# A fixed order for every engine in the MLP's down projection, with its loads issued by ScalarE

## The chip, the cores and the metric

The kernel runs on one core of a Trainium2 chip. A core has TensorE (PE in the profile: matmuls; PEld: the loads of its stationary operand), VectorE (DVE), ScalarE (ACT), GpSimd (POOL) and SyncE (SP), each with its own stream of instructions, and 16 DMA engines that move data between DRAM and the on-chip memories. The metric is the device time of one execution in microseconds (us).

## The reference, cut to what matters

A hybrid decoder block on x of 512 tokens by 2048 channels in float32: a token mixer (gated linear attention and differential attention, one output projection), then a gated MLP with a causal convolution, with norms around both. The change touches the MLP alone.

```python
def conv_ffn(h, w_ffn_in, conv_w, conv_b, w_ffn_out):        # D_FF = 5632
    up = h @ w_ffn_in                                        # 2048 -> 2 * 5632
    a, b = up[..., :D_FF], up[..., D_FF:]
    a = (conv_w[0] * a_pad[:, 0:S] + conv_w[1] * a_pad[:, 1:S + 1]
         + conv_w[2] * a_pad[:, 2:S + 2] + conv_b)
    return (jax.nn.gelu(a, approximate=True) * b) @ w_ffn_out   # 5632 -> 2048

h = rmsnorm(x, ffn_pre_norm[l])
f = conv_ffn(h, w_ffn_in[l], conv_w[l], conv_b[l], w_ffn_out[l])
x = x + rmsnorm(f, ffn_post_norm[l])
```

## The kernel before, in words

**Products of float32 in three matmuls.** A matmul reads fp32r, a rounded float32. Each operand is therefore two fp32r numbers, hi (the rounded value) and lo (what the rounding left), and a product is hi·hi + hi·lo + lo·hi. Weights pass through in *granules*: a block of 128 x 1024 float32 (512 KB) is loaded into a buffer named `raw` or `rt` (four of each), ACT copies it to hi (L136) and DVE subtracts to get lo (L137). The hi and lo go to one of three slots of a tile named `ring`, or to a pair named `xhi`, `xlo`, which every fourth granule of the down projection uses. `ring` has two placements, LEVEL and APART, which shift the halves by some columns; a half in one placement reaches into the neighbour's slot in the other. The up projection uses APART, the down projection LEVEL. Activations are split the same way by ACT and DVE (L149, L150) into pieces of the tiles `ah` and `al`.

**Seven products for eight.** Hidden channels come in eleven groups of 512. Of each pair of groups 2c+1 and 2c+2 (c = 0 to 4), the down projection is computed as 2 x 2 block products in the Strassen and Winograd form: seven products where eight would be. A *unit* is one pair c and one half `cb` of the output columns, so there are ten of them, `downs[0]` to `downs[9]`. The segments of a unit are called x0, z0, y0, z1, x1, y1, y2; each has two granules of 12 matmuls of 128 x 512 (L1024 to L1026). The units overlap: the order of segments is x0 of the next unit ahead of y2 of this one, and its z0 behind. The up projection is made of such units too (L927 to L929, matmuls of 128 x 256).

The sums that the form needs are made on the way. Of weights: the block loaded as `t` feeds x0 and z0 (and gets another block added by an accumulating DMA that POOL issues, L876), then DVE adds `b22` (L892) for y0, and `b21` (L910) for y2; `b22` feeds z1 and, after another accumulating DMA, y1; `b21` feeds x1. Of activations: DVE makes four sums of a finished pair of groups (`token_sums`, L995), SP stores them and three plain quarters to DRAM (`sd0s`, `sd0a` for pair 0, and so on), and `prepare` loads each back into a tile `st` and splits it. The names of these seven are a11, s5, s2, s3, a12, s7, a22, in the order of the segments x0, z0, y0, z1, x1, y1, y2.

Each segment's result is added from PSUM to `acc` or `accp` in SBUF by DVE (L1032), or written by ACT for the first pair (L1030). After the last unit six operations of 128 x 1024 (L1119) add `accp` into `acc`. The eleventh group (group 0, computed first, kept in DRAM as `ud0`) has no partner; its down projection is 16 plain parts of 12 matmuls (L1139 to L1141) at the end, each added (L1143), squared (L1148), scaled (L1152), and the rows are finished with the norm and the residual (L1172). The residual is loaded from `x1d`, 4 MB in four pieces, into `ah` and `al` once these are free.

**What sets the order.** The code calls the segments of the units in order; the framework's scheduler places the instructions on each engine by a simulated timeline and by the order of the code. All loads (`raw`, `rt`, `st`) are issued by SP (L48), and SP's order, too, is the scheduler's. Only the last parts of the last group stand in an order written out by hand, inside `tc.manual_schedule(engines=IN_ORDER)`, where PE, ACT, DVE and POOL take their instructions as the code emits them.

Of the kernel before, what the change touches and what calls it, by code (L numbers as in the profile page):

```python
# [17 lines left out]
P = 128  # L18
# [17 lines left out]
def hybrid_layer(ctx: ExitStack, tc: tile.TileContext, x, attn_pre_norm, w_in, w_alpha_up, b_alpha,  # L36
# [813 lines left out]
    def load_t(src, a):  # L850
        raw = rp.tile([P, GR], F32, name="rt", tag="rt", bufs=4)
        dma(raw.rearrange("p (a b) -> p a b", a=a), src)
        return raw
# [77 lines left out]
    held = {}  # L931

    def up_unit(gi, br):
# [10 lines left out]
        def out(seg, b):  # L944
# [20 lines left out]
            elif seg == "y2":  # L965
                tt(st["u0"][:, :, T[1]], v, st["p1"], ALU.add)
                if br == 0:
                    activate(0)
                else:
                    product(0)  # L970
                    token_sums(gi, st["u0"], st["u1"])
# [13 lines left out]
    def token_sums(gi, u0, u1):  # L985
        c, i = (gi - 1) // 2, (gi - 1) % 2
        T = [slice(0, 256), slice(256, 512)]
        a11, a21, a12, a22 = u0[:, :, T[0]], u0[:, :, T[1]], u1[:, :, T[0]], u1[:, :, T[1]]

# [3 lines left out]
        def add(n, x, y, op):  # L993
            t = fp.tile([P, 2, 256], F32, name=n, tag="sum", bufs=2)
            tt(t, x, y, op)  # L995
            put(n, t)
            return t
# [4 lines left out]
        s5 = add("s5", a21, a22, ALU.subtract)  # L1002
        s2 = add("s2", s5, a11, ALU.subtract)
        add("s7", a11, a21, ALU.subtract)
        add("s3", s2, a12, ALU.add)
# [50 lines left out]
    for i, u in enumerate(ups):  # L1056
        nxt = ups[i + 1] if i + 1 < len(ups) else None
        if i == 0:
# [4 lines left out]
        if i == 0:  # L1063
            for h, r in enumerate(s7raw):
                split(up["s7"][0][:, h], up["s7"][1][:, h], r)
        if nxt is None:
            prepare(0, "a11")
        u.x1()
        if nxt is None:
            prepare(0, "s5")  # L1070
        u.y1()
        if nxt is not None:
            nxt.x0()
            u.y2()
            nxt.z0()
        else:
            downs = [down_unit(c, cb) for c in range(NG // 2) for cb in range(2)]
            downs[0].x0()
            prepare(0, "s2")
            u.y2()  # L1080
    accps = large_tile("accp")
    accp = [accps[:, :D // 2], accps[:, D // 2:]]
    acc = [large_tile(f"acc{t}") for t in (2, 3, 0, 1)]
    acc = acc[2:] + acc[:2]
    ssf = [few.tile([P, 4], F32, name=f"ssf{t}") for t in range(NT)]
    downs[0].z0()
    extra[0] = True
    for i, u in enumerate(downs):
        nxt = downs[i + 1] if i + 1 < len(downs) else None
        nc_ = (i + 1) // 2  # L1090
        first = i % 2 == 0
        last_cb = i % 2 == 1 and nxt is not None

        if first:
            prepare(i // 2, "s3")
        if i == 6:
            g3 = large_tile("g3")
            bcast_row(g3, ffn_post_norm[0])
        u.y0()
        if first:  # L1100
            prepare(i // 2, "a12")
        u.z1()
        if first:
            prepare(i // 2, "s7")
        u.x1()
        if first:
            prepare(i // 2, "a22")
        if last_cb:
            prepare(nc_, "a11")
        u.y1()  # L1110
        if last_cb:
            prepare(nc_, "s5")
        if nxt is not None:
            nxt.x0()
        else:
            for j in range(2):
                for half, c, op in ((1, 0, ALU.add), (1, 1, ALU.subtract), (0, 1, ALU.subtract)):
                    dst = acc[2 * half + j].rearrange("p (b c x) -> p b c x", b=2, c=2)[:, :, c, :]
                    tt(dst, dst, accp[j].rearrange("p (b x) -> p b x", b=2), op)  # L1119
        if last_cb:  # L1120
            prepare(nc_, "s2")
        u.y2()
        if nxt is not None:
            nxt.z0()

    place_w[0] = LEVEL


# [115 lines left out]
```

## Time and profile before

| | |
|---|---|
| median of 3 runs | 2150.28 us (2150.27 to 2150.32) |
| the profiled execution | 2150.54 us |
| its span, first to last instruction | 2148.8 us |
| mean granted TensorE clock | 0.997 |
| PE busy | 2108.8 us, 98% of the span |
| DVE busy | 1415.8 us, 66% |
| ACT busy | 900.2 us, 42% |
| POOL busy | 199.2 us, 9% |

All times below are counted from the span's start. The up projection ends and the down projection begins at about 1690 us; the down units run from there to about 2088, the last group's parts to about 2140, and the finishing of the rows to 2148.8. A row that ends in brackets says how long the engine was idle just before the instruction and what ended that idle time. A wait for several things is put down to the one that came last.

### The profile page before, as it was taken

What the parts mean: (1) busy time and instruction counts of PE and PEld (TensorE: products, weight loads), DVE (VectorE), ACT (ScalarE), POOL (GpSimd) and SP (SyncE); (2) the same over time, 40 slices, a digit from 0 to 9 for tenths busy, and PEclk for the clock granted to TensorE, in tenths of its full rate; (3) what the DMA queues carried; (4) which work ended last, traced back from release to release, by engine and by line L of the source; (5) the groups of instructions that cost most, each with busy time, mean ns of one, the idle gap of its engine ahead of it and who ended that gap; (6) DMA issues with size and microseconds to landing.
All of it is one profiled execution on the core that took longest, in us unless ns stands there. A gap on an engine that the chain in (4) does not pass through costs nothing.

```text
span 2148.8 us, 31859 instructions
## 1 busy us (share of the span) xinstructions
PE 2108.8 (98%) x13009; PEld 1874.8 (87%) x13009; DVE 1415.8 (66%) x1725; ACT 900.2 (42%) x1162; POOL 199.2 (9%) x242
## 2 busy tenths in 40 slices
PE   7999999999999999999999999999999899999998
PEld 6878888888888888899999999999999778887886
DVE  5345554443444237688778786787877778888887
ACT  4233332333343224344544553554454555444433
POOL 1000000000000001010111101111011111111100
PEclk9999999999999999999999999999999999999999
DMA  6322222223224235356775767758577777676653
GB/s 214 102 72 79 79 70 79 79 79 88 78 80 170 95 128 186 119 118 143 167 182 132 169 162 173 167 136 194 142 171 183 189 216 207 168 196 175 160 166 144
DMA packets 218471, 303.83 MB, mean 141 GB/s; under 512 B 11776, under 2 KB 155572, under 8 KB 216404
## 3 DMA queue, kind: packets, MB, share of 16 engines
q1 hardware_dynamic: 165204, 238.87, 33.2%
q0 software_dynamic: 53120, 62.92, 19.1%
q8 instruction: 102, 1.67, 0.3%
q14 instruction: 45, 0.37, 0.1%
HBM read 273.97 MB, written 27.79 MB: 140 GB/s over the span
## 4 chain that ended last, share of the span: by engine, by line
PE 54%; issue 37%; DMA 3%; POOL 3%; DVE 2%; ACT 1%; POOLq 0%; SPq 0%; DVEq 0%; ACTq 0%
PE bank L190 7%; PE bank L191 7%; PE bank L192 7%; PE bank L174 5%; PE bank L172 5%; PE bank L173 5%; PE bank L929 4%; PE bank L927 4%; PE bank L928 4%; POOL rt L876 2%; POOL raw L876 1%; PE bank L440 1%; DMA raw<-in_w_ffn_in_dram 1%; PE bank L508 1%; PE bank L539 1%
## 5 line engine op out<-in xcount | busy, mean ns | idle before, releaser
L137 DVE TENSOR_TENSOR ring<-raw,ring 128x1024 fp32r<-128x1024 f32 x305 | 371.7, 1221 | 354.0 <-ACT ring L136 349.6
L136 ACT ACTIVATE ring<-raw 128x1024 fp32r<-128x1024 f32 x305 | 322.7, 1060 | 594.2 <-PE bank L192 157.2
L929 PE MATMUL bank<-ah,ring 128*128 128x256 f32 x1280 | 353.5, 276 | 0.7 <-DVE ring L137 0.7
L927 PE MATMUL bank<-ah,ring 128*128 128x256 f32 x1280 | 353.3, 276 | 0.0
L928 PE MATMUL bank<-al,ring 128*128 128x256 f32 x1280 | 353.3, 276 | 0.0
L137 DVE TENSOR_TENSOR ring<-rt,ring 128x1024 fp32r<-128x1024 f32 x221 | 269.3, 1221 | 92.3 <-ACT ring L136 92.2
L136 ACT ACTIVATE ring<-rt 128x1024 fp32r<-128x1024 f32 x221 | 233.5, 1060 | 223.5 <-PE bank L928 151.5
L929 PEld LDWEIGHTS bank<-ah,ring 128*128 128x128 f32 x1280 | 240.3, 188 | 1.1 <-DVE ring L137 1.1
L928 PEld LDWEIGHTS bank<-al,ring 128*128 128x128 f32 x1280 | 240.3, 188 | 0.1
L927 PEld LDWEIGHTS bank<-ah,ring 128*128 128x128 f32 x1280 | 240.3, 188 | 0.1
L190 PE MATMUL bank<-ring,ah 128*128 128x512 f32 x600 | 236.9, 398 | 0.2 <-ACT ah L149 0.2
L191 PE MATMUL bank<-ring,ah 128*128 128x512 f32 x600 | 235.9, 394 | 0.0
L192 PE MATMUL bank<-ring,al 128*128 128x512 f32 x600 | 235.1, 394 | 0.0
L172 PE MATMUL bank<-ah,ring 128*128 128x512 f32 (+1 forms) x512 | 195.9, 383 | 1.9 <-ACT ring L136 1.9
L174 PE MATMUL bank<-ah,ring 128*128 128x512 f32 (+1 forms) x512 | 194.2, 380 | 0.0
L173 PE MATMUL bank<-al,ring 128*128 128x512 f32 (+1 forms) x512 | 194.1, 379 | 0.0
L1025 PE MATMUL bank<-ring,ah 128*128 128x512 f32 x424 | 166.7, 393 | 8.8 <-DVE ring L137 8.8
L1026 PE MATMUL bank<-ring,al 128*128 128x512 f32 x424 | 165.8, 391 | 0.0
L1024 PE MATMUL bank<-ring,ah 128*128 128x512 f32 x424 | 158.2, 391 | 2.4 <-ACT ring L136 2.1
L192 PEld LDWEIGHTS bank<-ring,al 128*128 128x128 f32 x600 | 113.2, 189 | 24.2 <-DVE al L150 0.3
L191 PEld LDWEIGHTS bank<-ring,ah 128*128 128x128 f32 x600 | 113.3, 189 | 23.8 <-DVE ring L137 0.5
L190 PEld LDWEIGHTS bank<-ring,ah 128*128 128x128 f32 x600 | 113.2, 189 | 23.7 <-ACT ah L149 0.6
(260 smaller groups left out, 4063.4 us busy)
## 6 DMA issues: line engine op xcount, KB each, us to landing
raw<-in_w_in_dram SPq DMA_DIRECT2D x96, 512.0 KB, 3.7
raw<-in_w_ffn_in_dram SPq DMA_DIRECT2D x96, 512.0 KB, 5.1
raw<-in_w_ffn_out_dram SPq DMA_DIRECT2D x48, 512.0 KB, 6.7
rt<-in_w_ffn_in_dram SPq DMA_DIRECT2D x40, 512.0 KB, 5.9
rt<-in_w_ffn_in_dram POOLq DMA_DIRECT2D x40, 512.0 KB, 6.2
raw<-in_w_ffn_in_dram POOLq DMA_DIRECT2D x40, 512.0 KB, 6.9
raw<-in_w_o_dram SPq DMA_DIRECT2D x32, 512.0 KB, 3.7
rt<-in_w_ffn_out_dram SPq DMA_DIRECT2D x20, 512.0 KB, 7.3
```

What stands on the lines that cost most here:

```text
L136: act(hi, raw, AF.Copy)
L137: tt(lo, raw, hi.bitcast(F32), ALU.subtract)
L172: mm(o, wh, ah[:, t0:t1, kk, :], start=st, stop=False)
L173: mm(o, wh, al[:, t0:t1, kk, :], start=False, stop=False)
L174: mm(o, wl, ah[:, t0:t1, kk, :], start=False, stop=sp)
L190: mm(banks[t], ah[:, t, s, :], w[0][:, k, :], start=st, stop=False)
L191: mm(banks[t], ah[:, t, s, :], w[1][:, k, :], start=False, stop=False)
L192: mm(banks[t], al[:, t, s, :], w[0][:, k, :], start=False, stop=sp)
L927: mm(o, wh, sh[:, :, kk, :], start=start and kk == 0 and n == 0, stop=False, **NOW)
L928: mm(o, wh, sl[:, :, kk, :], start=False, stop=False, **NOW)
L929: mm(o, wl, sh[:, :, kk, :], start=False, stop=kk == HK - 1, **NOW)
L1025: mm(b[j], sh[:, o:o + P], w[1][:, q, :], start=False, stop=False, **NOW)
```

## The change

From the last up unit's x1 on, through all ten down units and two of the last group's 16 parts, everything is emitted by a new function, `run_in_order`, inside `manual_schedule(IN_ORDER)`. It walks over a list of granules; before the matmuls of granule i it makes the halves of all granules up to two ahead (i < 10) or three ahead (from then on), and behind the matmuls it calls what `hooks` holds for that granule: loads, sums, splits, the combination. What was a method of a unit (`x0` to `y2`, `more`) is now a place in that table. In detail:

- Loads of `t` (L852), `b22` and `b21` (L102) from the second down unit on, and loads of `st` (L1101) from the second pair on, are issued by ACT, one per granule. Those of the first unit and the first pair stay on SP.
- `prepare` falls into two steps, the load and the split, each with its own granule. Those of a11 and s5 of the first pair are called ahead of the region.
- The last `token_sums` is spread over four granules of the first down unit (L1002 now).
- The six combining operations become twelve of half the width (still L1119), half of them inside the last unit and half behind it.
- The loads and splits of the last group's activations move up, to units 4 and 5 and to the last unit. The weights of its first parts are made inside the region, and its first two parts stand ahead of the last y2.
- `ring` changes from APART to LEVEL once, at a granule where the spare pair lies between the two.
- `b21` of the last up unit is loaded ahead of the region.

The core of the diff:

```diff
-    def load(src, a):
+    def load(src, a, by=None):
         raw = wpool.tile([P, GR], F32, name="raw", tag="raw", bufs=4)
-        dma(raw.rearrange("p (a b) -> p a b", a=a), src)
+        (by or nc.sync).dma_start(out=raw.rearrange("p (a b) -> p a b", a=a), in_=src)
...
+    def prepare_parts(c, n, by):
+        got = []
+
+        def first():
+            got.append(small_tile("st"))
+            by.dma_start(out=got[0], in_=sd[c][n].rearrange("p g x -> p (g x)"))
+
+        def second():
+            split(piece(ah, *place[n]), piece(al, *place[n]), got[0])
...
+    def run_in_order(u, order, ahead):
+        gran = [(v, seg, g) for v, seg in order for g in range(2)]
+        ready, nxt = {}, [0]
...
+        def make(i):
+            v, seg, g = gran[i]
+            turn[0] += 1
+            place_w[0] = APART if i < late else LEVEL
+            if v is None:
+                gr0.append(ffn_out_granule(0, 0, g, extra[i]))
+                return
+            raw = getattr(v, SOURCE[seg][1])[g]
+            ready[i] = granule(None, v.a, raw, spare=extra[i])
+            j = {"x0": 1, "z1": 1}.get(seg)
+            if j:
+                nc.gpsimd.dma_start(out=raw.rearrange("p (a b) -> p a b", a=v.a), in_=v.block(0, j, g),
+                                    accum_op=ALU.add)
+
+        for i, (v, seg, g) in enumerate(gran):
+            while nxt[0] < len(gran) and nxt[0] <= i + (1 if nxt[0] == late else ahead(i)):
+                make(nxt[0])
+                nxt[0] += 1
+            if v is None:
+                for t in range(2 * g):
+                    ffn_out_part(whole, gr0, t, 0)
+                continue
+            op = SOURCE[seg][0]
+            if g == 0 and seg[1] == "0":
+                v.banks[seg[0]] = v.chain(seg[0])
+            v.prods(v.banks[seg[0]], op, g, ready.pop(i), seg[1] == "0")
+            if g:
+                v.out(seg, v.banks[seg[0]])
+            for f in hooks.pop((v, seg, g), ()):
+                f()
...
+        for d, v in enumerate(downs):
+            order += [(v, s) for s in ("z0", "y0", "z1", "x1", "y1")]
+            order += [(downs[d + 1], "x0") if d + 1 < len(downs) else (None, "last"), (v, "y2")]
...
+            for w, name, where in ((nxt, "t", (("z0", 0), ("y0", 1))), (nxt, "b22", (("x1", 0), ("x1", 1))),
+                                   (v if d else None, "b21", (("y2", 0), ("y2", 1)))):
+                for g in range(2) if w else ():
+                    at(before if name == "b21" else v, *where[g], lambda w=w, name=name, g=g: load_g(w, name, g, nc.scalar))
...
+    with tc.manual_schedule(engines=IN_ORDER):
+        run_in_order(u, order, lambda i: 2 if i < 10 else 3)
+    for k in range(3):
+        combine(1, k)()
```

What this does to the engines' orders is seen at three places. The first is SP's order where the up projection passes into the down projection; `st<-sd0s` are the loads of s5, s2, s3, s7 (in before the first of them is s5's), `st<-sd0a` those of a11, a12, a22. Before:

```order
L48 DMA raw<-in_w_ffn_in_dram 128x4x256 x2
L48 DMA rt<-in_w_ffn_out_dram 128x2x512 x2
L48 DMA st<-sd0a_6404 128x1024
L48 DMA raw<-in_w_ffn_out_dram 128x2x512 x4
L48 DMA st<-sd0s_6407 128x1024
L48 DMA st<-sd0s_6408 128x1024
L48 DMA st<-sd0s_6410 128x1024
L48 DMA st<-sd0a_6405 128x1024
```

The same place in the changed kernel:

```order
L102 DMA raw<-in_w_ffn_in_dram 128x4x256 x2
L852 DMA rt<-in_w_ffn_out_dram 128x2x512 x2
L48 DMA st<-sd0a_6404 128x1024
L48 DMA st<-sd0s_6407 128x1024
L1101 DMA st<-sd0s_6408 128x1024
L102 DMA raw<-in_w_ffn_out_dram 128x2x512 x2
L1101 DMA st<-sd0s_6410 128x1024
L102 DMA raw<-in_w_ffn_out_dram 128x2x512 x2
L1101 DMA st<-sd0s_6409 128x1024
```

The first two loads from `sd0s` moved from behind the four loads of down weights to ahead of them, and the later ones stand between these.

The second is DVE's order at the same passage; L137 makes a weight's lo half, L150 the lo half of a piece of the activations, L953, L955, L960 work on the up projection's result `u`, and L980 (L985 in the changed kernel) makes its product. Before, from the first split of a11 on:

```order
L150 TENSOR_TENSOR al<-st,ah 128x1024
L953 SCALAR_TENSOR_TENSOR u<-bank,p_14674 128x2x256
L137 TENSOR_TENSOR ring<-raw,ring 128x1024 x2
L955 TENSOR_TENSOR u<-u,bank 128x2x256
L137 TENSOR_TENSOR ring<-raw,ring 128x1024 x2
L137 TENSOR_TENSOR ring<-rt,ring 128x1024
L150 TENSOR_TENSOR al<-st,ah 128x1024
L137 TENSOR_TENSOR ring<-rt,ring 128x1024
L960 TENSOR_TENSOR u<-u,bank 128x2x256
L150 TENSOR_TENSOR al<-st,ah 128x1024
L980 TENSOR_TENSOR u<-u 128x1024
```

The changed kernel, from the same split on:

```order
L150 TENSOR_TENSOR al<-st,ah 128x1024
L953 SCALAR_TENSOR_TENSOR u<-bank,p_14674 128x2x256
L150 TENSOR_TENSOR al<-st,ah 128x1024
L137 TENSOR_TENSOR ring<-raw,ring 128x1024 x2
L955 TENSOR_TENSOR u<-u,bank 128x2x256
L137 TENSOR_TENSOR ring<-raw,ring 128x1024 x2
L1094 TENSOR_TENSOR rt<-rt,raw 128x1024 x2
L137 TENSOR_TENSOR ring<-rt,ring 128x1024
L150 TENSOR_TENSOR al<-st,ah 128x1024
L137 TENSOR_TENSOR ring<-rt,ring 128x1024
L960 TENSOR_TENSOR u<-u,bank 128x2x256
L985 TENSOR_TENSOR u<-u 128x1024
```

The second split (s5's) moved from between the lo halves of down weights (`ring<-rt`, the two granules of x0) to ahead of four lo halves of the up projection's last weights; two weight sums (L1094, L910 in before) now stand ahead of the first down granule, and a split (s2's) stands where s5's was.

The third is ACT's order in a steady unit. Before, it held copies alone:

```order
L149 ACTIVATE ah<-st 128x1024
L136 ACTIVATE ring<-rt 128x1024
L136 ACTIVATE ring<-raw 128x1024
L136 ACTIVATE xhi<-raw 128x1024
L136 ACTIVATE ring<-raw 128x1024 x3
L136 ACTIVATE xhi<-raw 128x1024
L136 ACTIVATE ring<-rt 128x1024 x3
```

In the changed kernel, near the start of the fifth pair, the loads stand between them:

```order
L136 ACTIVATE ring<-rt 128x1024 x2
L149 ACTIVATE ah<-st 128x1024
L1101 DMA st<-sd4a_6433 128x1024
L136 ACTIVATE ring<-rt 128x1024
L1101 DMA st<-sd4s_6437 128x1024
L136 ACTIVATE xhi<-rt 128x1024
L102 DMA raw<-in_w_ffn_out_dram 128x2x512
L136 ACTIVATE ring<-rt 128x1024
L102 DMA raw<-in_w_ffn_out_dram 128x2x512
L136 ACTIVATE ring<-rt 128x1024
L149 ACTIVATE ah<-st 128x1024
L852 DMA rt<-in_w_ffn_out_dram 128x2x512
```

Each of these loads waits, on ACT, until its buffer is free, and the copies behind it wait with it. At the end of SP's order the loads of `x1d_4800` and `x1d_4801` (2 MB) now stand directly ahead of the last group's weight loads: in before six `raw` loads of down weights, among them the last group's first, stood ahead of that pair.

More of the change, by code (lines that the diff above doesn't have):

```diff
@@ L848, in hybrid_layer, with load_t @@
     drain()
[L850 removed]
+    def load_t(src, a, by=None):
         raw = rp.tile([P, GR], F32, name="rt", tag="rt", bufs=4)
[L852 removed]
+        (by or nc.sync).dma_start(out=raw.rearrange("p (a b) -> p a b", a=a), in_=src)
         return raw
@@ L1066, in hybrid_layer @@
         if nxt is None:
-            prepare(0, "a11")
+            break
         u.x1()
-        if nxt is None:
-            prepare(0, "s5")
         u.y1()
[L1072 to L1082, printed above, removed]
```

193 lines of the change are left out of this document (127 added, 66 removed).

## The prediction

> **What bounds the kernel now.** I read the page's first part, then the windows by stage, then the idle time of the engine that is nearly always busy, then the rows of the engines it waited for.
>
> ```profile
> PE   2108.8 (98%) x13009; PEld 1874.8 (87%) x13009; DVE 1415.8 (66%) x1725; ACT 900.2 (42%) x1162; POOL 199.2 (9%) x242
> ```
> ```profile
> 1676.00:1690.00 14.00, 14.00 (x126) 14.00 (x125) 8.17 (x8) 5.79 (x6) 1.29 (x1) 1.00 0.99 243
> 1690.00:1740.00 50.00, 39.94 (x186) 31.91 (x185) 36.39 (x35) 24.36 (x28) 5.88 (x5) 0.93 0.89 260
> 1740.00:1777.00 37.00, 37.00 (x165) 30.64 (x164) 28.71 (x27) 24.29 (x29) 4.49 (x5) 1.00 0.71 190
> 1740.00:2088.00 348.00, 346.49 (x1523) 284.96 (x1522) 295.96 (x312) 166.34 (x169) 41.40 (x36) 1.00 0.68 177
> 2088.00:2149.00 61.00, 50.38 (x218) 40.25 (x216) 45.36 (x66) 18.46 (x39) 2.96 (x8) 0.96 0.40 149
> ```
>
> The span is 2148.8 us and PE is busy for 2108.8 of it, so all of PE's idle time is 40.0 us, and no matmul is added or removed. The second fence (us from the span's start, then length, then busy us and instructions of PE, PEld, DVE, ACT, POOL, then granted clock, DMA share, GB/s) covers the region of the change. PE is idle for 10.06 us in the 50 us of the passage from the up to the down projection, 1.51 us in the 348 us of the down projection, and 10.62 us at the end. A row with no gap in it (1740 to 1777, 165 matmuls) gives the cadence, 0.224 us per 512-wide matmul; 12 make a granule, 2.7 us, and 14 granules a unit, 37 us.
>
> ```profile
> PE bank L1025 <- DVE ring L137: 8.0, 3, 5.5
> PE bank L1024 <- ACT ring L136: 2.1, 3, 1.0
> ```
> ```profile
> 1678.79 6.62 SPq L48 DMA_DIRECT2D raw<-in_w_ffn_out_dram  x4
> 1685.46 10.09 SPq L48 DMA_DIRECT2D st<-sd0s  x3
> ```
> ```profile
> 1692.89 1.06 ACT L149 ACTIVATE ah<-st 128x1024 fp32r<-128x1024 f32 x1 [4.21 <-DMA st<-sd0s]
> ```
> ```profile
> 1688.72 1.23 DVE L137 TENSOR_TENSOR ring<-rt,ring 128x1024 fp32r<-128x1024 f32 x1 [3.70 <-ACT ring L136]
> 1693.98 1.23 DVE L150 TENSOR_TENSOR al<-st,ah 128x1024 fp32r<-128x1024 f32 x1 [4.04 <-ACT ah L149]
> 1695.12 1.22 DVE L137 TENSOR_TENSOR ring<-rt,ring 128x1024 fp32r<-128x1024 f32 x1
> ```
> ```profile
> 1696.99 0.63 PE L1026 MATMUL bank<-ring,al 128*128 128x512 f32 x1
> ...
> 1700.40 0.48 PE L1026 MATMUL bank<-ring,al 128*128 128x512 f32 x1
> ```
>
> These are PE's waits from 1560 to 1760 (us, times, longest), then SP's, ACT's, DVE's and PE's rows in the passage. The longest wait, 5.5 us, names a weight's lo half (L137), but that subtraction waited for nothing of its own: it starts at 1695.12 because the split before it in DVE's order (L150 at 1693.98) sat 4.04 us for ACT's half, which sat 4.21 us for the load of `s5` from `sd0s`. SP issued that load at 1685.46, behind four weight loads in its order, and it took 1692.89 − 1685.46 = 7.4 us. After the wait eight matmuls start in 1700.40 − 1696.99 = 3.41 us, 0.43 each and not 0.224; with the one at 1696.40, nine cost 1.9 us more, the clock's share of the wait. The Trainium skill, "TensorE: Matmul & The Clock Gate", Part 1, says that the clock halves after an idle window of about 3.4 us and returns after about as long a busy one; the row at 0.93 and these starts agree.
>
> A matmul's record lasts about 0.17 us beyond the next one's start, so each separate wait hides that much: with seven in the passage, 10.06 + 1.9 + 7 × 0.17 = 13.2 us are lost there. The same for the down projection, with about five waits: 1.51 + 0.85 = 2.4 us.
>
> ```profile
> PE bank L1025 <- DVE ring L137: 0.8, 2, 0.5
> PE bank L1140 <- DVE xlo L137: 0.8, 1, 0.8
> PE bank L1025 <- DVE xlo L137: 0.4, 2, 0.2
> PE bank L1140 <- DVE ring L137: 0.3, 1, 0.3
> PE bank L1024 <- DVE acc L1032: 0.3, 1, 0.3
> ```
>
> These are PE's waits from 1760 on; the two on L1140 belong to the last group, 1.1 us and with what is hidden 1.5. The rest of the 10.62 is the tail behind the last matmul.
>
> **The change, part by part.**
>
> *The passage.* The `s5` load goes out ahead of the raw loads that it stood behind, and its two splits stand in DVE's order ahead of the last up unit's x1, no longer between the halves of the first down granules. Both links of the chain above go: −13.2 us. What is late next: DVE.
>
> ```profile
> 1711.69 1.22 DVE L980 TENSOR_TENSOR u<-u 128x1024 f32<-128x1024 f32 x1
> 1715.47 0.69 DVE L995 TENSOR_TENSOR s<-u 128x512 f32<-128x512 f32 x1
> ```
>
> The windows give 36.39 us of DVE work in 50, and the same work (products and splits at 1.22, sums at 0.69) now has to fit beside a lo of 1.22 in every 2.7 us. Counting it off granule by granule, the up unit's x1 is short by about 0.3 us and the first y0 by 0.8 and 0.4: +1.5 us. From below this is 0 (all of it fits); from above 5, one wait like the old one without the half clock. I take 1.5. The ring's two placements, whose shifted buffers overlap, no longer alternate in the passage; the waits that this caused are among the seven, and the one switch left is part of the 1.5.
>
> *The steady units.*
>
> ```profile
> 2088.71 1.28 DVE L1032 TENSOR_TENSOR acc<-acc,bank 128x512 f32<-128x512 f32 x2
> 2089.91 2.35 DVE L1119 TENSOR_TENSOR acc<-acc,accp 128x1024 f32<-128x1024 f32 x2
> ```
>
> Per granule DVE does one lo (1.22), one output (L1032, 1.28 / 2 = 0.64) and the rest in splits and adds. Over the unit that is the 28.7 us of 37 in the row, and the new order deals it out so that no granule has over 3.5 us and the backlog never passes 0.9 us. Halves are made three granules ahead: 3 × 2.7 − 1.06 − 1.22 = 5.8 us of lead. So −2.4 us of waits goes and I leave 0.4 for what a queue in fixed order can't step around: −2.0. Ends: −2.4, and no gain.
>
> *Loads issued by ScalarE.* Seven `st` loads per two units and six weight loads per unit make 9.5 issues in 37 us. No row of before has a DMA issued by ACT; the nearest are SP's and POOL's:
>
> ```profile
> 2096.66 0.34 SPq L48 DMA_DIRECT2D ah<-x1d  x1
> ...
> 2097.88 2.43 SPq L48 DMA_DIRECT2D raw<-in_w_ffn_out_dram  x2
> ```
> ```profile
> L876 POOL DMA_DIRECT2D rt<-in_w_ffn_out_dram x20: 1170/1192/1202, 1690.3 to 2049.4; - x20
> ```
>
> At SP's 0.34 this is 3.2 us of ACT per unit, at POOL's 1.19 it is 11.3. ACT's 24.29 of 37 in the row (the densest) becomes 27.5 or 35.6: hidden at either end, so 0. If the cover is gone (ACT late by more than the 5.8 us of lead), it is rival C. I take SP's, since both issue plain loads. Each load also waits on ACT for its buffer, with the next hi queued behind it; the buffer's last reader stands at least one granule earlier in the order, so I price that at 0 too. The Trainium skill, "DMA: Bandwidth & Descriptors", "Issuing engines are not separate DMA queues", speaks against a gain from this part: all issuers share 16 engines, and another one saves only the sequencer's time. By that the part alone gives 0, as I have it.
>
> *POOL's accumulating loads* keep their number and 1.19 us each; POOL is busy 4.49 of 37, and they now follow the hi and lo that release them in a fixed order: 0. *The final combination* (L1119, six of 1.18) becomes twelve pieces of 512 at 0.64, half of them spread over the last unit: +0.6 us of DVE work, where the unit has some 6 spare: 0. *The last group's activations* are loaded and split earlier, 2 × 1.22 us for DVE in two units: 0. *Matmuls, bytes, tail:* the same.
>
> *The end.* Two of the last group's 16 parts move ahead of the last y2. Their two weight loads (and the ones after) stand in SP's order behind the first `x1d` pair, 2 MB, which waits until the last unit's z1 has been read, time T.
>
> ```profile
> 2077.93 0.42 SPq L48 DMA_DIRECT2D ah<-x1d  x1
> 2079.62 14.17 SPq L48 DMA_DIRECT2D raw<-in_w_ffn_out_dram  x4
> ```
> ```profile
> 2103.91 2.21 ACT L136 ACTIVATE ring<-raw 128x1024 fp32r<-128x1024 f32 x2
> ```
>
> In before the raw issued at 2097.88, behind the other pair, was ready for ACT some 7 to 8 us later (the next hi's start at 2103.91 and 2.21 us long). With T + 1.2 for three issues and 8 us, the first block lands near T + 9.3, its hi ends at T + 10.4 and its lo at T + 11.7. PE needs them after x1 and y1, four granules or T + 10.8: about 0.8 us. The second block's lo stands behind two outputs and a split on DVE and ends near T + 15.2, needed at T + 13: 2.2 more. Two later blocks give up to 1: about 3.7 in all with the hidden part, against 1.5 in before: +2.2 us. From below −1.5 (all the old waits go), from above +5 (both blocks 8 us late in a row).
>
> **Sum**, against the profiled execution's 2150.5 us (its span and 1.7 around it): −13.2 + 1.5 − 2.0 + 2.2 = −11.5, so 2139.0; the median of the runs, 2150.3, lies 0.3 below the profiled one: 2138.7.
>
> **Rivals.**
> A. *All covered.* The DVE squeeze and the late last blocks cost nothing: −13.2 − 2.4 − 1.5 = −17.1, so 2133.2. For it: ACT and DVE have 13 and 8 us free per unit; against: the 2 MB ahead of the last weights.
> B. *The late transfer changes its name.* The `st` loads go ahead, so 1 MB more stands before the down weights, at 260 GB/s (the row) 3.8 us; DMA share is 0.89 to 0.99 there, the densest of the kernel. If DVE is squeezed as well, 4 to 5 us remain, and one wait over 4 us brings back 1.9 of half clock: 2138.7 + 6 = 2145. The same price holds if it is the end's wait that grows. By the skill's rule on shared engines above, this is what one would expect if transfer, not order, was late.
> C. *Slower: ACT held up by its own loads.* A load that waits for its buffer stops the hi's behind it. Once ACT is late by more than 5.8 us in a unit, PE waits there in each of nine units; it decides from 11.6 / 9 = 1.3 us per unit on, and 2 us gives 2138.7 + 18 = 2157. For it: `st` loads took 7.4 us above, and in fixed order nobody steps around. Against: the loads stand four or more granules (10.7 us) ahead of their use.
> D. *It doesn't reach the wait:* the old wait stays under another order, 2150.
>
> **How the numbers follow.** Forecast 0.50, A 0.17, B 0.18, C 0.11, D 0.04. The likeliest is 2138.7. The range goes from A to B's middle: 2132.5 to 2146; left out are C, D and the worst of B. Within 0.2% (4.3 us, about what can be told from no change) lies D: 0.04; slower is C: 0.11; faster the rest, 0.85.
>
> **What would show it.** PE's busy time from 1690 to 1740 near 48 us at a granted clock of 1.00; no wait over 3 us on L137 in the passage; ACT's loads at about 0.35 us; no wait of over 0.5 us per unit in the steady units; a wait of 1 to 3 us on the last group's first blocks. Wrong: ACT idle behind a load's buffer, PE waiting for a hi once per unit, or a window with the clock below 0.95.

## The result, and the profile after

The changed kernel is slower: 2158.91 us median (2156.41 to 2160.19, 5 runs) beside 2150.27 us (2145.62 to 2150.32, 5 runs), a ratio of 1.0047 with a 95% interval of 1.0033 to 1.0062. The forecast was 2138.7 us. The profiled execution, the fastest of the five, took 2156.41 us with a span of 2154.7, 5.9 us longer than the span before; the traces below explain these 5.9 us, and the medians lie 8.6 apart. One single slow run of an experiment further down, of 4940.18 us where the kernel's other nine took 2153.59 to 2160.88, is left out of its median.

The windows of the changed kernel over the same three stages, columns as in the prediction:

```profile
PE   2111.9 (98%) x13009; PEld 1872.2 (87%) x13009; DVE 1415.6 (66%) x1731; ACT 895.8 (42%) x1162; POOL 199.2 (9%) x242
...
1690.00:1740.00 50.00, 48.90 (x237) 40.44 (x236) 36.87 (x37) 25.57 (x31) 5.40 (x5) 1.00 0.83 219
1740.00:2090.00 350.00, 339.69 (x1466) 272.91 (x1465) 286.21 (x304) 155.08 (x161) 40.21 (x34) 1.00 0.70 180
2090.00:2155.00 65.00, 50.56 (x216) 40.23 (x216) 50.36 (x73) 21.47 (x43) 2.96 (x8) 0.95 0.37 138
```

The passage is repaired: PE busy for 48.90 of 50 us where it was 39.94, and the clock stays at 1.00. But the down projection, which stood idle for 1.51 us in 348, is now idle for 10.31 in 350, and the clock is full: these are many short waits. PE's waits there (1740 to 2088) and behind it (2086 to 2150):

```profile
PE bank L1030 <- DVE ring L137: 3.8, 7, 0.8
PE bank L1030 <- DVE xlo L137: 2.6, 4, 0.8
PE bank L1029 <- DVE acc L1037: 2.4, 9, 0.8
PE bank L1029 <- ACT ring L136: 0.7, 1, 0.7
```
```profile
PE bank L1261 <- DVE xlo L137: 2.6, 2, 1.8
PE bank L1261 <- DVE ring L137: 1.5, 2, 0.8
PE bank L1260 <- ACT ring L136: 0.8, 1, 0.8
```

Where the time went can be counted without a remainder. All matmuls are in both traces (1680 of the ten units, 192 of the last group), so each segment of each unit can be found by counting, and its loss is the time from its first matmul to the next segment's first, less its matmuls at full pace (0.227 us each for 512 columns: the rows below start 48 matmuls apart; 0.1135 for 256).

```profile
2131.46 0.39 PE L1261 MATMUL bank<-ring,ah 128*128 128x512 f32 x1
...
2142.34 0.39 PE L1261 MATMUL bank<-xlo,ah 128*128 128x512 f32 x1
```

| us lost | before | after | difference |
|---|---|---|---|
| passage: d0 and the last up unit's y2 | 13.9 | 2.1 | −11.8 |
| units d1 to d9 | 2.7 | 17.7 | +15.0 |
| last group's matmuls | 2.2 | 5.5 | +3.3 |
| from the last matmul on | 9.6 | 10.1 | +0.5 |
| first down matmul starts at | 1690.3 | 1689.2 | −1.1 |
| sum | | | +5.9 |

(In before, too, the scheduler had put one of the last group's parts ahead of d9's y2; the 0.4 us lost there are counted with the last group.)

In d1 to d9 most of the loss has one place: y0 of eight of the nine units loses 0.8 to 1.6 us each, 11.4 in all, and z0 ahead of it another 2.3. The other 4 us lie at x1 and y1 of d1, d5 and d9, and about 0.1 us each at most units' z1. d9 loses nothing at y0. This is the place in a unit (d6), DVE first, then ACT, PE and POOL:

```profile
1940.62 1.28 DVE L1037 TENSOR_TENSOR accp<-accp,bank 128x512 f32<-128x512 f32 x2
1942.01 1.23 DVE L137 TENSOR_TENSOR xlo<-rt,xhi 128x1024 fp32r<-128x1024 f32 x1
1943.15 1.22 DVE L1094 TENSOR_TENSOR rt<-rt,raw 128x1024 f32<-128x1024 f32 x1
1945.58 1.22 DVE L137 TENSOR_TENSOR ring<-rt,ring 128x1024 fp32r<-128x1024 f32 x1 [1.21 <-ACT ring L136]
1946.72 1.28 DVE L1037 TENSOR_TENSOR acc<-acc,bank 128x512 f32<-128x512 f32 x2
1947.91 1.22 DVE L1094 TENSOR_TENSOR rt<-rt,raw 128x1024 f32<-128x1024 f32 x1
1950.34 1.22 DVE L137 TENSOR_TENSOR ring<-rt,ring 128x1024 fp32r<-128x1024 f32 x1 [1.21 <-ACT ring L136]
```
```profile
1940.91 1.06 ACT L136 ACTIVATE xhi<-rt 128x1024 fp32r<-128x1024 f32 x1 [1.47 <-DMA rt<-in_w_ffn_out_dram]
1940.93 0.39 ACTq L102 DMA_DIRECT2D raw<-in_w_ffn_out_dram  x1
1944.48 1.06 ACT L136 ACTIVATE ring<-rt 128x1024 fp32r<-128x1024 f32 x1 [2.51 <-DVE rt L1094]
1949.25 1.06 ACT L136 ACTIVATE ring<-rt 128x1024 fp32r<-128x1024 f32 x1 [3.71 <-DVE rt L1094]
```
```profile
1951.62 0.50 PE L1030 MATMUL bank<-ring,ah 128*128 128x512 f32 x1 [0.77 <-DVE ring L137]
```
```profile
1930.47 1.17 POOL L1171 DMA_DIRECT2D rt<-in_w_ffn_out_dram  x1 [13.63 <-DVE ring L137]
1932.80 1.19 POOL L1171 DMA_DIRECT2D rt<-in_w_ffn_out_dram  x1 [1.16 <-DVE xlo L137]
```

It is a chain through one pair of buffers, the blocks `t`. The second accumulating load, issued at 1932.80, lands when ACT's hi begins, at 1940.91, 8.1 us later. Then, each behind the last: hi and lo of z0's second granule, the sum t + b22 of the first granule (1943.15), its hi on ACT (1944.48), for which DVE sits idle for 1.21 us, its lo, the output of y2, the second sum (1947.91), its hi on ACT, again 1.21 us of idle DVE, its lo. The last lo ends at 1951.56, 10.7 us after the landing, and PE has waited for it. The output of y2 (1946.72) that stands in the same chain frees the PSUM bank that PE takes next; that is the wait on L1037. In before the scheduler had put the first sum *ahead* of z0's second lo, into the wait for the landing. There the same place, d8, DVE and then ACT:

```profile
2018.63 1.28 DVE L1032 TENSOR_TENSOR accp<-accp,bank 128x512 f32<-128x512 f32 x2
2019.83 1.22 DVE L892 TENSOR_TENSOR rt<-rt,raw 128x1024 f32<-128x1024 f32 x1
2022.68 1.22 DVE L137 TENSOR_TENSOR xlo<-rt,xhi 128x1024 fp32r<-128x1024 f32 x1 [1.64 <-ACT xhi L136]
2023.82 1.22 DVE L137 TENSOR_TENSOR ring<-rt,ring 128x1024 fp32r<-128x1024 f32 x1
```
```profile
2021.59 1.06 ACT L136 ACTIVATE xhi<-rt 128x1024 fp32r<-128x1024 f32 x1 [4.13 <-DMA rt<-in_w_ffn_out_dram]
```

With the sum done at 2021.05, y0's first hi and lo follow z0's at once, without idle time between them; this unit's y0 loses 0.8 us, and six of the nine lose under 0.1.

### The profile page after: what moved, and what is told of

Read it like the earlier page. It is cut to its first block, busy times and chain, and to the rows that moved or that the text cites. A ratio compares the mean times of both kernels' runs of the same rounds, so it can differ in the third digit from the quotient of the medians.

```text
span 2154.7 us, 31761 instructions
## 1 busy us (share of the span) xinstructions
PE 2111.9 (98%) x13009; PEld 1872.2 (87%) x13009; DVE 1415.6 (66%) x1731; ACT 895.8 (42%) x1162; POOL 199.2 (9%) x242
## 4 chain that ended last, share of the span: by engine, by line
PE 56%; issue 34%; DVE 3%; POOL 3%; DMA 2%; ACT 1%; POOLq 0%; SPq 0%; DVEq 0%; ACTq 0%
PE bank L190 7%; PE bank L191 7%; PE bank L192 7%; PE bank L929 5%; PE bank L927 5%; PE bank L928 5%; PE bank L174 5%; PE bank L172 5%; PE bank L173 5%; PE bank L440 1%; DVE ring L137 1%; POOL raw L1171 1%; PE bank L508 1%; DMA raw<-in_w_ffn_out_dram 1%; PE bank L539 1%
## 5 line engine op out<-in xcount | busy, mean ns | idle before, releaser
L137 DVE TENSOR_TENSOR ring<-raw,ring 128x1024 fp32r<-128x1024 f32 x304 | 371.2, 1223 | 366.1 <-ACT ring L136 358.3
L927 PE MATMUL bank<-ah,ring 128*128 128x256 f32 x1280 | 353.3, 276 | 0.0
L137 DVE TENSOR_TENSOR ring<-rt,ring 128x1024 fp32r<-128x1024 f32 x222 | 271.1, 1222 | 99.7 <-ACT ring L136 97.5
L927 PEld LDWEIGHTS bank<-ah,ring 128*128 128x128 f32 x1280 | 240.3, 188 | 0.1
L190 PE MATMUL bank<-ring,ah 128*128 128x512 f32 x600 | 237.1, 398 | 0.5 <-ACT ah L149 0.5
L191 PE MATMUL bank<-ring,ah 128*128 128x512 f32 x600 | 235.9, 394 | 0.0
L1030 PE MATMUL bank<-ring,ah 128*128 128x512 f32 x428 | 167.8, 392 | 4.9 <-DVE ring L137 4.9
L1029 PE MATMUL bank<-ring,ah 128*128 128x512 f32 x428 | 168.2, 393 | 3.4 <-DVE acc L1037 2.4
```

Of the source, the lines that this page charges most:

```text
L137: tt(lo, raw, hi.bitcast(F32), ALU.subtract)
L190: mm(banks[t], ah[:, t, s, :], w[0][:, k, :], start=st, stop=False)
L191: mm(banks[t], ah[:, t, s, :], w[1][:, k, :], start=False, stop=False)
L927: mm(o, wh, sh[:, :, kk, :], start=start and kk == 0 and n == 0, stop=False, **NOW)
L1029: mm(b[j], sh[:, o:o + P], w[0][:, q, :], start=start and st == 0, stop=False, **NOW)
```

## The experiments

Theory 1 is that chain in DVE's order. Theory 2 is the prediction's own rival, that ACT is held up by the loads that it issues. Theory 3 is that DVE has too much work around y0. All times are medians of 4 to 10 runs; what a unit or the passage loses is counted in the one profiled execution. The kernel before, run beside them on the same chips, had medians of 2150.0 to 2152.9 us, but single runs from 2146.0 to 2156.7; ratios are given with their intervals for that reason.

**The sums one granule earlier.**

```diff
-            for g in range(2):
-                at(before, "y2", g, lambda v=v, g=g: add_t(v, "b22", g))
+            for g, where in enumerate(((v, "x0", 1), (before, "y2", 0))):
+                at(*where, lambda v=v, g=g: add_t(v, "b22", g))
```

> The changed kernel with the two weight sums t + b22 of a unit one granule earlier each: the first behind x0's second granule (ahead of the lo half of z0's second granule in DVE's order), the second behind y2's first granule (ahead of y0's first lo half). Same work. Theory 1 (a chain in DVE's order: landing of the second accumulating load, z0's lo, sum, hi, lo, output, sum, hi, lo of y0, with DVE idle for 1.2 us twice while ACT makes a hi): the waits at y0, 1.2 to 1.6 us a unit, go, the nine units lose under 5 us instead of 17.7, and the time falls by about 12 us to 2146. Theory 2 (ACT is held up by the loads that it issues): nothing changes, 2159. Theory 3 (DVE has too much to do around y0, in whatever order): nothing changes, 2158 to 2160.

2138.48 us, a ratio of 0.9944 (0.9926 to 0.9961) to before, 20 us under the changed kernel. From 1740 to 2070 PE has no wait at all. In the first unit, where halves are made two ahead, the sum now stood ahead of z0's halves, so that unit's z0 is computed from other weights and its passage (3.8 us lost) says nothing. Theories 2 and 3 fall: the same loads on ACT, the same work on DVE. Not all of the 20 us are the units', though: the last group loses 2.3 us here and not 5.5, for another reason (see its first weights below).

**The same from the second unit on.**

```diff
+            for g, where in enumerate(((v, "x0", 1), (before, "y2", 0)) if d else ((u, "y2", 0), (u, "y2", 1))):
+                at(*where, lambda v=v, g=g: add_t(v, "b22", g))
```

> As the earlier run with the sums t + b22 one granule earlier, but from the second down unit on alone; in the first one they stay where the changed kernel has them. Theory 1: the units d1 to d9 lose under 2 us instead of 17.7 and the passage stays near 2 us: 2138 to 2143 us. Theory 3 (too much work for DVE): the units lose 10 us or more once the first unit's sums are in their place, 2150 or more.

2137.52 us (2134.06 to 2138.35), 0.9926 (0.9900 to 0.9951): under the lowest that theory 1 gave. Windows of the steady units and DVE's rows at the place (d6):

```profile
1740.00:2070.00 330.00, 330.00 (x1458) 273.25 (x1457) 291.34 (x308) 162.75 (x165) 40.21 (x34) 1.00 0.73 187
```
```profile
1927.59 1.27 DVE L1037 TENSOR_TENSOR accp<-accp,bank 128x512 f32<-128x512 f32 x2
1928.79 1.22 DVE L1094 TENSOR_TENSOR rt<-rt,raw 128x1024 f32<-128x1024 f32 x1
1930.44 1.23 DVE L137 TENSOR_TENSOR xlo<-rt,xhi 128x1024 fp32r<-128x1024 f32 x1 [0.44 <-ACT xhi L136]
1931.70 1.23 DVE L1094 TENSOR_TENSOR rt<-rt,raw 128x1024 f32<-128x1024 f32 x1
1932.85 1.22 DVE L137 TENSOR_TENSOR ring<-rt,ring 128x1024 fp32r<-128x1024 f32 x1
```

PE is busy for 330.00 of 330.00 us, with DVE busy for 291.34 of them. The changed kernel has 1381 matmuls in the same stretch (its row is shown further down), 77 fewer, or 17.5 us at 0.227, close to the table's 17.7. The last group loses 2.2 us.

**Half of that move.** The second sum directly behind the first, both still behind the landing:

```diff
             for g in range(2):
-                at(before, "y2", g, lambda v=v, g=g: add_t(v, "b22", g))
+                at(before, "y2", 0, lambda v=v, g=g: add_t(v, "b22", g))
```

> The changed kernel with the second of the two sums t + b22 moved up to stand directly behind the first one (both behind the lo half of z0's second granule, ahead of y0's first lo). Against the first experiment, the wait for the second accumulating load still stands ahead of both sums; only the two idle times of 1.2 us, in which DVE waits for ACT's hi, are filled. If these idle times are what the 1.6 us at y0 are made of, d1 to d9 lose under 4 us instead of 17.7: 2140 to 2145. If the place behind the landing matters as much, 6 to 10 us are left: 2146 to 2151.

2143.53 us, 0.9971 (0.9960 to 0.9982). d1 to d9 lose 5.7 us, between the two answers on record (the time is the first answer's, because the last group loses 3.3 us less as well). So 12 of the 17.7 go with the second sum's place, which fills DVE's two idle times, and the rest hangs on the first sum's place behind the landing, which is all in which these steady units differ from those of the early sums. (In the first unit the second sum again runs ahead of a half of z0, which then has other weights.) Waits from 1740 to 2090:

```profile
PE bank L1029 <- DVE acc L1037: 2.4, 4, 1.2
PE bank L1030 <- DVE ring L137: 0.7, 1, 0.7
```

**Without the landing.**

```diff
-            if j:
+            if j and seg != "x0":
                 nc.gpsimd.dma_start(out=raw.rearrange("p (a b) -> p a b", a=v.a), in_=v.block(0, j, g),
```

> The changed kernel without the accumulating loads onto the blocks t (20 of the 40 of POOL's in the down projection), so z0 and what follows from t get weights that lack a term; all other work is the same, sums, halves and ACT's loads too. Theory 1: the chain now starts when z0's halves have a free slot, 3 to 8 us earlier, the waits at y0 go and the nine units lose under 5 us: about 2145. Theory 2: ACT issues as many loads as before, the waits stay: 2157 to 2159. Theory 3: DVE has the same work, the waits stay: 2157 to 2159.

2139.66 us, 0.9956 (0.9941 to 0.9971); d1 to d9 lose 2.5 us. With the sums where the changed kernel has them, taking the chain's start away is nearly enough (it also takes 10 MB of transfers away, which the kernels with the early sums kept). The last group loses 7.1 us here, so the time is not lower still. The same is seen inside the changed kernel in d9, beside which fewer loads run: POOL's second load was issued at 2052.51 and ACT's hi begins at 2058.83, 6.3 us later and not 8.1, and y0 loses nothing, though DVE has the same two idle times of 1.21 us there.

```profile
2052.51 1.19 POOL L1171 DMA_DIRECT2D rt<-in_w_ffn_out_dram  x1 [1.15 <-DVE ring L137]
```
```profile
2058.83 1.06 ACT L136 ACTIVATE ring<-rt 128x1024 fp32r<-128x1024 f32 x1 [1.73 <-DMA rt<-in_w_ffn_out_dram]
```

**The loads back on SP.** `nc.scalar` becomes `nc.sync` at both places that issue loads, from the same points of the code; where they stand in SP's order is then again the scheduler's choice:

```diff
-                    at(before if name == "b21" else v, *where[g], lambda w=w, name=name, g=g: load_g(w, name, g, nc.scalar))
+                    at(before if name == "b21" else v, *where[g], lambda w=w, name=name, g=g: load_g(w, name, g, nc.sync))
```

> The changed kernel with every load that ACT issues given back to SP, from the same places in the code. Theory 1: the chain at y0 stays, the nine units lose 15 to 20 us, 2157 to 2161. Theory 2: with the loads gone from ACT the waits at y0 go, 2143 to 2147. Theory 3: as theory 1. If SP's order brings back the old kind of wait (a small load behind loads that wait for a buffer), there are new waits of over 2 us on loads of st and the time is above 2162.

2169.49 us, 1.0094 (1.0079 to 1.0109), 10.6 us over the changed kernel: the time of the third answer without its wait, for between 1740 and 2070 ACT waits for no load of `st`. d1 to d9 lose 24.5 us, the passage 6.9, the last group 7.0. What grew in d1 to d9 is z0, which loses 11.1 us in all where it lost 2.3. The windows, the changed kernel's first:

```profile
1740.00:2070.00 330.00, 320.20 (x1381) 257.17 (x1381) 270.11 (x285) 149.59 (x156) 37.85 (x32) 1.00 0.69 176
```
```profile
1740.00:2070.00 330.00, 314.75 (x1348) 250.45 (x1347) 261.12 (x275) 146.99 (x154) 37.85 (x32) 1.00 0.66 172
```
```profile
1943.73 1.19 POOL L1171 DMA_DIRECT2D rt<-in_w_ffn_out_dram  x1 [1.16 <-DVE xlo L137]
```
```profile
1953.27 1.06 ACT L136 ACTIVATE xhi<-rt 128x1024 fp32r<-128x1024 f32 x1 [4.36 <-DMA rt<-in_w_ffn_out_dram]
```

The last two rows are this kernel's accumulating load in d6: 1943.73 to 1953.27, 9.5 us and not 8.1. Between those two times SP issued one load into `st` and two into `rt`, 512 KB each; in the changed kernel ACT issues one into `st` in that time, and the next two stand behind the landing. Over d1 to d9 the second accumulating load took 9.9 us (median) and not 8.6. That it is longer because of the loads beside it is likely, but no run changed this alone.

**The loads on SP, with the sums early.** Both edits together.

> The sums one granule earlier from the second unit on, and all loads of ACT given back to SP. With the loads on SP the changed kernel lost 24.5 us in d1 to d9 against 17.7. If the loads on ACT matter only through the chain at y0 (they keep the accumulating load's landing at 8 and not 9.4 us), the shorter chain hides that too: d1 to d9 lose under 3 us, 2139 to 2146. If SP's order costs by itself (loads behind others that wait for a buffer), d1 to d9 lose 6 us or more and the time is 2147 or more.

2142.73 us, 0.9957 (0.9942 to 0.9972). d1 loses 2.5 us and d2 to d9 nothing, so the shorter chain hides SP's loads too, as the first answer has it; the 5.2 us over the kernel with ACT's loads lie in the passage (6.1 us lost, 2.8 there) and in d1.

**The last group's first weights.** Loaded by ACT into the two `rt` buffers that are free in the last unit, with the sums early:

```diff
+        for g, where in enumerate(((f, "z0", 0), (f, "y0", 1))):
+            at(*where, lambda g=g: gr0_raw.append(load_t(w_y3[:, 2 * g:2 * g + 2, 0:512], 2, nc.scalar)))
...
-                gr0.append(ffn_out_granule(0, 0, g, extra[i]))
+                gr0.append(granule(None, 2, gr0_raw[g], spare=extra[i]))
```

> The run above, and the two weight blocks of the last group's first parts loaded by ACT into the free rt buffers during the last unit's z0 and y0, so that they no longer stand behind the 2 MB of x1d. If the end's wait comes from the place of these loads, the last group loses 2.3 us or less in each run and the time is 0 to 3 us under the run above: 2136 to 2141. If the two late pairs of blocks behind them set the end, there is no change.

2136.40 us (2135.23 to 2139.11), 0.9926 (0.9905 to 0.9947): the same as without it. The last group lost 2.2 us in both. In the kernel with the early sums the scheduler had already put the first of these loads ahead of `x1d`, so there was nothing left to gain. What the changed kernel's two late blocks cost by their place alone was not isolated, but the kernels above divide by it: where both loads stand behind the first pair of `x1d`, the last group loses 5.5 us (the changed kernel), 7.0 (loads on SP) and 7.1 (without the landing); where SP's order has the first of them ahead of it, 2.2 to 2.3 (the early sums, both kernels; half of the move; loads on SP with the sums early). The scheduler chose that order each time, and some 3 us of what these kernels gain go with it and not with the units.

**The passage.** Four kernels took the kernel before and moved only parts. First, the load and split of s5 alone:

```diff
         if nxt is None:
             prepare(0, "a11")
+            prepare(0, "s5")
         u.x1()
-        if nxt is None:
-            prepare(0, "s5")
```

> The kernel before with one call moved: the load and split of s5 for the first pair ahead of the last up unit's x1, so that its load stands ahead of the four weight loads in SP's order; everything else still ordered by the scheduler. If the 5.5 us wait and the half clock behind it come from that load's place alone, the passage loses 3 to 6 us instead of 13.9 and the time is 2140 to 2143. If the next late thing takes its place (s2's load still stands behind the four weight loads), the passage still loses 9 us or more and the time is 2146 to 2150.

2156.72 us, 1.0032 (1.0020 to 1.0044); the passage loses 16.8 us: the second answer, with a time above its range. The next split, s2's, stands where s5's stood, and its load is late in turn:

```profile
1692.18 2.25 ACT L149 ACTIVATE ah<-st 128x1024 fp32r<-128x1024 f32 x2 [3.78 <-DMA st<-sd0s]
```

Then four loads and splits ahead of x1 (`prepare` of s5, s2, s3, a12):

> The kernel before with the loads and splits of s5, s2, s3 and a12 of the first pair ahead of the last up unit's x1, so that no small load that the passage needs stands behind the four weight loads. With s5's alone the next split took the place of the old one and the passage lost 16.8 us. If it is the place of these loads, the passage now loses 2 to 6 us instead of 13.9 and the time is 2138 to 2143. If the passage's wait is another's (the accumulating loads, the ring's two placements), it loses 8 us or more: 2145 to 2152.

2159.30 us, 1.0033 (1.0019 to 1.0048), 10.6 us lost. This run says nothing on the loads: these splits overwrite pieces of `ah` and `al` that the last up unit still reads, so it computes from other activations, and PE now waits for the splits in the up projection itself (L927 for ACT's L149, 3.5 us once). So next, the loads of s5, s2 and s3 ahead, the splits called where they were:

```diff
         if nxt is None:
             prepare(0, "a11")
+            for n in ("s5", "s2", "s3"):
+                load_st(0, n)
         u.x1()
```

> The kernel before with the loads alone of s5, s2 and s3 of the first pair ahead of the last up unit's x1 (so ahead of the four weight loads in SP's order), and their splits called where they were. If the passage's long wait is that of these loads behind the weight loads, no wait over 3 us is left there, the passage loses 4 to 8 us instead of 13.9, and the time is 2141 to 2146. If it is another wait that the loads only cover, it loses 11 us or more: 2148 to 2152.

2153.69 us, 1.0011 (0.9999 to 1.0023), 13.2 us lost. At x0 the loss falls to 1.8 us (it was 7.8), but now s7's load, the next one left behind weight loads, holds up a split ahead of z0's halves, and z0 loses 6.3 us:

```profile
1701.19 1.06 ACT L149 ACTIVATE ah<-st 128x1024 fp32r<-128x1024 f32 x1 [4.45 <-DMA st<-sd0s]
```

Last, SP's order cleared, and DVE's left as it was: the loads b22 and b21 of the first down unit issued by POOL.

```diff
+            downs[0].by = nc.gpsimd
             downs[0].x0()
```

> The kernel before with one thing taken from SP's order: the four weight loads b22 and b21 of the first down unit, behind which the loads of s5, s2, s3 and a12 stood, are issued by POOL. DVE's order through the passage is word for word that of before. If the passage's waits are those of small loads held up in SP's order by weight loads that wait for buffers, no wait over 3 us is left at x0, the passage loses 3 to 7 us instead of 13.9, and the time is 2139 to 2145. If they come from the place of the splits in DVE's order, whatever SP does, it loses 10 us or more: 2147 or more.

2146.57 us, 0.9977 (0.9966 to 0.9988). No wait over 2.1 us is left, and x0 loses 1.7 us where it lost 7.8, with DVE's order unchanged: that long wait was SP's order. But the passage still loses 10.6 us, which is the second answer's loss, so neither answer holds whole. 5.3 of it are lost at z0. PE's waits from 1660 to 1760, then its rows at z0 and the window around them:

```profile
PE bank L1026 <- DVE ring L137: 3.8, 3, 2.1
PE bank L1025 <- ACT ring L136: 1.5, 3, 1.0
```
```profile
1702.64 0.73 PE L1025 MATMUL bank<-ring,ah 128*128 128x512 f32 x2 [1.03 <-ACT ring L136]
1705.51 0.79 PE L1026 MATMUL bank<-ring,ah 128*128 128x512 f32 x1 [2.14 <-DVE ring L137]
1706.10 0.63 PE L1027 MATMUL bank<-ring,al 128*128 128x512 f32 x1
...
1711.22 0.44 PE L1025 MATMUL bank<-ring,ah 128*128 128x512 f32 x1
```
```profile
1700.00:1710.00 10.00, 6.83 (x28) 5.23 (x27) 9.42 (x9) 3.13 (x4) 1.16 (x1) 0.72 0.91 253
```

So the half clock came back without a long wait: behind two waits of 1.03 and 2.14 us with two matmuls between them, twelve starts from 1706.10 to 1711.22 lie 0.43 us apart (the granted clock from 1700 to 1710 is 0.72), and that alone is 2.4 us of z0's 5.3. Which of the small waits has which cause stays open.

And from the other side, the good kernel (the sums early from the second unit on) with s5's and s2's loads put back behind weight loads, and their splits put back to later places in DVE's order:

```diff
-        prepare_at(0, "s2", (u, "x1", 0), (u, "y1", 0))
+        prepare_at(0, "s5", (u, "x1", 1), (u, "y1", 0))
+        prepare_at(0, "s2", (u, "x1", 1), (u, "y1", 1))
```

> The kernel with the sums one granule earlier from the second unit on (2137.5 us), with the loads of s5 and s2 of the first pair put back behind weight loads in SP's order, and s5's split put back between the lo halves of x0's two granules. If the passage's gain is that of these places, a wait of 4 to 7 us at x0 and the half clock come back, the passage loses 8 to 14 us instead of 2.8, and the time is 2143 to 2149. If the gain was another part of the fixed order, the passage stays under 5 us and the time under 2140.

2142.81 us, 0.9972 (0.9960 to 0.9983): 5.3 us worse than with them in place, 8.2 us lost in the passage, with a wait of 3.0 us and a granted clock of 0.83 from 1700 to 1710. So of the 11.8 us that the fixed order gains in the passage, some 5 hang on these two loads and their splits together; how the rest divides between the other splits, the sums and the ring's placement stays open.

## Why the prediction was wrong

- **What bounds the kernel and the passage: right in size, narrower in cause.** 13.2 us were read from the trace and 1.5 left; counted, it was 13.9 and 2.1, a gain of 11.8 for a forecast of 11.7. The step that "both links of the chain above go" was true, but the runs show that taking that load's lateness away alone gains 5 us at most (SP's order cleared) and otherwise nothing: as soon as s5 is early, s2 or s7 is the late one. No part that was tried by itself did what the whole order of the passage does. The prediction traces only the longest wait to its cause and names the ring's placements, without a row, for others; so that all 13.2 but 2.1 went is in part luck.
- **The steady units: the step that failed.** It read "the new order deals it out so that no granule has over 3.5 us and the backlog never passes 0.9 us", and concluded −2.0 us. It measured +15.0. The count was of DVE's *work* per granule. It left out what DVE waits for in that order: twice 1.21 us per unit in which it sits idle until ACT has made a hi, and the wait for the landing, which stands ahead of both sums. The 5.8 us of lead hold for a block that already lies in its buffer. For `t` there is no such lead: the same buffer is loaded, accumulated, split, summed and split again, and from the landing on that is a chain of 10.7 us. The early sums, which take the 17.7 us of d1 to d9 away with the same work, show it.
- **"The backlog" and DVE's share.** With PE busy all the time, DVE works for 291 of 330 us in the good kernel, more than the 270 in the changed one. Its share was no sign of a bound.
- **Loads issued by ScalarE: priced right, and worth more than the 0 given.** The rows have 0.35 to 0.39 us each, close to the 0.34 taken, and the rows at 1940.91 and 1940.93 above show the issue beside a running copy. Rival C, ACT held up by its loads, was wrong in its mechanism, though its sign and its place ("PE waits there in each of nine units", from 1.3 us per unit on) came true by another one; that its 2157 lies so near to the result is luck. Given back to SP the loads cost 10.6 us in this order and 5.2 in the good one. The Trainium skill, "DMA: Bandwidth & Descriptors", "Issuing engines are not separate DMA queues", says that another issuer saves only its sequencer's time; here the measurement differs by these 10.6 and 5.2 us. That the issuer's order decides when a load starts, and beside which others it runs, fits the rows in d6, but no run isolated it.
- **The end: right in direction, undersized.** 3.7 us expected, 5.5 measured (+3.3 and not +2.2). The two parts moved ahead lost 3.2 us, near the 0.8 and 2.2 that were priced; the later blocks lost 2.2, where up to 1 was. The tail grew by 0.5 and not by 0.
- **The clock: right here, under a condition that is too narrow.** No half clock appears in the passage, and the row at 1.00 stands where 0.93 stood. But rival B has it come back with "one wait over 4 us", and with SP's order cleared it came back behind waits of 1.03 and 2.14 us. How much idle time in how long a stretch it takes, these runs don't settle.
- **Two readings that are a little off.** The cadence of 0.224 us is a window's count with the matmuls at both edges in it; rows 48 apart give 0.227, so a unit takes 38.1 us and not 37. And the waits shown for the passage are six, not seven. Neither moves the forecast by more than 0.2 us.
- **The chances.** The 0.11 for slower held one mechanism. No case held "the fixed order puts one instruction behind the wrong wait in every unit", though a walk of one whole unit, from landing to lo, with each engine's order and the rows of the trace, would have given it.

## What to carry to other kernels

When an order is written by hand, don't check it by counting work per step: walk the longest chain through one buffer, from its last DMA's landing to the last instruction that needs it, and put into every wait of that chain the work that doesn't depend on it. A sum that is ready before a landing belongs ahead of the instruction that waits for the landing; here one granule's difference in place took the 17.7 us that d1 to d9 lost down to nothing. (The time fell by 21 us, from 2158.9 to 2137.5; some 3 of them go with SP's order at the end.) And when a stall is removed by moving the late thing, look for the next thing in the same queue: twice here it took the same place.

## What the runs showed of the hardware that was not expected

ACT's DMA issues did not lengthen its copies: the issue at 1940.93 (0.39 us) runs while the copy that began at 1940.91 is under way, and that copy takes 1.06 us like the one at 2021.59 in before, where ACT issues no loads. Loads of 512 KB issued by ACT, mostly one at a time, landed in 3.7 us (median of 36), while SP's loads of the same matrix took 6.7 in before and 5.0 in the changed kernel with its loads back on SP (medians of 48), and POOL's accumulating ones 8.0:

```profile
raw<-in_w_ffn_out_dram ACTq DMA_DIRECT2D x36, 512.0 KB, 3.7
...
rt<-in_w_ffn_out_dram POOLq DMA_DIRECT2D x20, 512.0 KB, 8.0
```

The half clock came back without any wait over 2.1 us, as shown above with SP's order cleared. The first down matmul started anywhere from 1687 to 1691 us in kernels that share all code ahead of it, and the kernel before spread over 10 us from run to run, much more than its first three runs showed.
